# Stacked gate weights, joined score matmuls, three value chunks and a spread recurrence in a hybrid decoder trunk

## The chip, the core and the metric

The kernel runs on one core of a Trainium2 chip. The metric is the device time of one execution in microseconds (us); lower is better. The core has TensorE (PE: matmuls, and PEld: the loads of their stationary operand), VectorE (DVE), ScalarE (ACT), GpSimd (POOL) and SyncE (SP), which issues nearly all transfers. Each engine runs its own instructions in their order and waits on semaphores for the others.

## The reference

Two layers over 256 tokens of 1024 features, all in float32. The stage that the change touches lies between two feed-forward blocks of 2816 hidden features:

```python
h = rms_norm(x, mix_norm[i])
rx, rgate, q, k, v, f_logit, ga, gb = jnp.split(h @ w_in[i], split_idx, axis=-1)
# branch A: recurrence (16 blocks of 64 features)
rx = causal_dwconv(rx, conv_w[i], conv_b[i])                  # 4 taps
r  = sigmoid(block_diag(rx, rg_wa) + rg_ba);  ig = sigmoid(block_diag(rx, rg_wx) + rg_bx)
a  = exp(-8 * r * softplus(-lambda));  u = sqrt(1 - a*a) * ig * rx
ya = (scan(a, u) * gelu(rgate)) @ w_rnn_out[i]                # h_t = a_t h_(t-1) + u_t
# branch B: 8 heads of 128, causal, with a cumulative forget bias
s  = (q . k) / sqrt(128) + dcum[query] - dcum[key]            # q, k normalised per head
yb = (softmax(s, causal) @ v) @ w_attn_out[i]
x  = x + (sigmoid(ga + mb_a) * ya + sigmoid(gb + mb_b) * yb) @ w_o[i]
```

## The kernel before

**Precision.** Every operand of a matmul is split in two rounded parts, high and low, and a product is the sum of three: high by high, high by low and low by high. `mm3` (lines 303 to 306) issues the three as single matmuls. For the largest projections `mm2` puts the activation's two parts side by side, 512 columns, so that the high weight meets both in one matmul and the low weight meets the high part in another (lines 344 to 347).

**Weights.** Class `Weights` walks a plan, one list of chunks for the whole program. A chunk of about 1 MB goes by one transfer on SyncE's queue into one of 3 raw buffers (line 84). It is cut in two units, and of each unit ScalarE makes the high part `wh` (line 95) and VectorE the low part `wl` (line 96), with 5 buffers for either. A call of `next()` hands out a unit and emits the pair four units ahead. A unit feeds some 2.8 us of matmuls. A later chunk of the plan needs a raw buffer that both its units' pairs have left.

**Order.** Work that may be late is put into a list (`defer`), and `tick()` takes steps from it between units. The program is then scheduled: instructions keep their dependencies, but the scheduler sets each engine's order by its own model of time, except where `keep_in_program_order` pins one.

**The mixing stage**, once per layer, in order of the plan:

1. Eight projections of the recurrence's input (`rx_post`, lines 511 to 524): a convolution of four taps on VectorE, then a split of the result into `xch` and `xcl` (lines 522, 523).
2. Values (lines 579 to 605): four chunks of 258 columns, 1024 values and the 8 forget logits together; for each chunk 8 feature tiles times 2 token tiles times 3 matmuls. Behind chunks two, three and four stand the block-diagonal matmuls of `gates` (lines 548 to 567), 2 gates times 3 matmuls for each of 8 feature tiles; tiles 5 to 7 stand within the next stage. Two tanh on ScalarE give the two gates. Step `s1` clamps one (line 559) and makes `a`, `th` and `a2`; `s2` forms the two factors of `u` on VectorE (lines 565, 566).
3. Queries and keys of heads 0 to 3 (`qk_group`, 16 matmuls of 512 columns times 3 for each of queries and keys), then, after a `drain`, one square root over all eight tiles (`root`, line 570), and queries and keys of heads 4 to 7. In its first four units the eight products and scans (`scan`, lines 575, 576) are called two by two.
4. 24 projections called fillers (`filler`, line 754 on): eight for the gelu, eight for merge gate A, eight for B, in that order. Between the units stand the steps of the attention: `step_a` transposes one head's queries and keys and splits them, `step_b` makes scores (lines 704 to 711) and softmax, `step_c` transposes the probabilities, `step_d` applies them to the values. The head h begins at slot 4 + (5h+1)//2, where slots 0 to 7 are the second queries-and-keys group and 8 to 31 the fillers.
5. The two output projections `ya` and `yb`, the merge, and `w_o`.

**Scores before.** Tokens are two blocks of 128. Block 0 sees 128 keys and block 1 sees 256; each takes three matmuls by `mm3` and a fourth that adds both forget biases, the query's and the key's, through an operand that ScalarE builds for each head (line 702). Scores carry the opposite sign, so softmax takes the minimum; a query's own bias shifts a whole row of scores.

## Time and profile before

| what | value |
|---|---|
| median of 3 runs | 1322.99 us (1322.97 to 1323.11) |
| the profiled execution's own time | 1323.63 us |
| its span, first to last instruction | 1321.8 us |
| mean granted TensorE clock | 0.997 of full |
| busy: PE, DVE, ACT | 1311.8, 1076.1, 815.5 us |
| matmuls | 8610 |
| mixing stages of the two layers, about | 198 to 413 and 850 to 1064 us |

A group row reads: line, engine, operation, written tile <- read tiles, shapes, count | busy us, mean ns of one | idle time of the engine ahead of it and who ended it. A row of stretches reads: from:to, length, then for PE, PEld, DVE, ACT and POOL the busy us (and instructions), the granted clock, the share of the DMA engines and GB/s. Matmuls overlap their successors, so the distance between two matmuls comes from start times and not from the length of one.

### The profile page before, as it was taken

How to read it: one execution, taken by the hardware profiler on the slowest of the kernel's cores; microseconds unless marked ns; L12 is line 12 of the kernel's file. 1: busy time of each engine (PE TensorE's matmuls, PEld its weight loads, DVE VectorE, ACT ScalarE, POOL GpSimd, SP SyncE). 2: the span in 40 equal slices, each digit the busy share in tenths (PEclk: the TensorE clock that was granted, in tenths of full speed). 3: DMA queues.
4: the chain of work that ended last, by engine and by line, in shares of the span. 5: the costliest groups of instructions: out<-in, count | busy, mean ns of one | idle time of the engine just before them, and what ended most of it. 6: DMA issues, size and time to landing. Idle time of an engine off the chain costs nothing.

```text
span 1321.8 us, 22442 instructions
## 1 busy us (share of the span) xinstructions
PE 1311.8 (99%) x8610; PEld 1197.7 (91%) x8610; DVE 1076.1 (81%) x2142; ACT 815.5 (62%) x1470; POOL 34.1 (3%) x43
## 2 busy tenths in 40 slices
PE   9999999999999999999999999999999999999997
PEld 8888899889999888889988888998999998888897
DVE  7998769899757899876789877698997678988756
ACT  6665656868655666565566555578677556655653
POOL 1000000020000000000000000000200000000000
PEclk9999999999999999999999999999999999999998
DMA  8654665445435555456545546644543455554650
GB/s 292 243 179 160 212 225 193 158 164 175 151 128 191 196 189 189 162 184 231 187 165 192 188 153 212 241 161 159 193 166 128 161 190 191 192 191 142 213 187 33
DMA packets 37259, 240.21 MB, mean 182 GB/s; under 512 B 4128, under 2 KB 4768, under 8 KB 14368
## 3 DMA queue, kind: packets, MB, share of 16 engines
q1 hardware_dynamic: 36720, 238.25, 51.3%
q8 instruction: 68, 1.11, 0.3%
q10 hardware_dynamic: 432, 0.52, 0.1%
q14 instruction: 39, 0.32, 0.1%
HBM read 237.71 MB, written 1.05 MB: 181 GB/s over the span
## 4 chain that ended last, share of the span: by engine, by line
PE 99%; DMA 0%; DVE 0%; ACT 0%; SPq 0%; POOLq 0%; issue 0%; DVEq 0%
PE mm L347 20%; PE mm L345 11%; PE at L347 11%; PE at L345 6%; PE f L304 3%; PE f L305 3%; PE f L306 3%; PE qk L309 2%; PE qk L311 2%; PE qk L310 2%; PE mm L306 2%; PE mm L304 2%; PE mm L305 2%; PE ya L347 2%; PE mm L344 2%; PE at L344 2%
## 5 line engine op out<-in xcount | busy, mean ns | idle before, releaser
L95 ACT ACTIVATE wh<-wr 128x1024 fp32r<-128x1024 f32 (+2 forms) x476 | 467.4, 986 | 308.0 <-PE mm L347 90.8
L96 DVE TENSOR_TENSOR wl<-wr,wh 128x1024 fp32r<-128x1024 f32 (+2 forms) x476 | 537.7, 1132 | 142.3 <-ACT wh L95 136.9
L347 PE MATMUL mm<-h,wh 128*128 128x512 f32 x616 | 219.2, 394 | 0.0
L347 PE MATMUL at<-h,wh 128*128 128x512 f32 x616 | 218.4, 394 | 0.0
L345 PE MATMUL mm<-h,wl 128*128 128x256 f32 x704 | 182.4, 281 | 0.0
L345 PE MATMUL at<-h,wl 128*128 128x256 f32 x704 | 181.7, 281 | 0.3 <-DVE wl L96 0.2
L347 PE MATMUL mm<-f,wh 128*128 128x512 f32 x504 | 176.8, 394 | 0.0
L345 PE MATMUL mm<-f,wl 128*128 128x256 f32 x528 | 144.0, 280 | 0.0
L345 PEld LDWEIGHTS at<-h,wl 128*128 128x128 f32 x704 | 131.8, 188 | 8.8 <-DVE wl L96 0.8
L345 PEld LDWEIGHTS mm<-h,wl 128*128 128x128 f32 x704 | 131.8, 188 | 7.8 <-DVE wl L96 0.4
L347 PEld LDWEIGHTS mm<-h,wh 128*128 128x128 f32 x616 | 115.6, 188 | 22.5
L347 PEld LDWEIGHTS at<-h,wh 128*128 128x128 f32 x616 | 114.9, 188 | 21.9
L347 PEld LDWEIGHTS mm<-f,wh 128*128 128x128 f32 x504 | 94.4, 188 | 20.8
L304 PE MATMUL f<-h,wh 128*128 128x256 f32 x384 | 108.6, 283 | 0.0
L306 PE MATMUL f<-h,wl 128*128 128x256 f32 x384 | 108.4, 282 | 0.0
L305 PE MATMUL f<-h,wh 128*128 128x256 f32 x384 | 108.4, 282 | 0.0
L345 PEld LDWEIGHTS mm<-f,wl 128*128 128x128 f32 x528 | 99.4, 188 | 2.1
L305 PEld LDWEIGHTS f<-h,wh 128*128 128x128 f32 x384 | 72.3, 188 | 0.1
L304 PEld LDWEIGHTS f<-h,wh 128*128 128x128 f32 x384 | 72.3, 188 | 0.1
L306 PEld LDWEIGHTS f<-h,wl 128*128 128x128 f32 x384 | 72.4, 189 | 0.0
L381 ACT ACTIVATE sum<-mm 128x256 f32<-128x256 f32 x112 | 40.2, 376 | 49.3 <-PE mm L347 49.3
L382 DVE TENSOR_TENSOR sum<-mm,sum 128x256 f32<-128x256 f32 x112 | 44.9, 417 | 15.0 <-ACT sum L381 15.0
(291 smaller groups left out, 2857.6 us busy)
## 6 DMA issues: line engine op xcount, KB each, us to landing
wr<-in_w2i SPq DMA_DIRECT2D x44, 1024.0 KB, 4.8
wr<-in_w1i SPq DMA_DIRECT2D x41, 1024.0 KB, 4.8
wr<-in_wf SPq DMA_DIRECT2D x32, 1024.0 KB, 4.8
wr<-in_w1o SPq DMA_DIRECT2D x32, 704.0 KB, 4.0
wr<-in_w2o SPq DMA_DIRECT2D x32, 704.0 KB, 4.0
wr<-in_wqk SPq DMA_DIRECT2D x16, 1024.0 KB, 4.8
wr<-in_wv SPq DMA_DIRECT2D x8, 1032.0 KB, 4.9
wr<-in_wro SPq DMA_DIRECT2D x8, 1024.0 KB, 4.8
```

Of the source, the lines that this page charges most:

```text
L95: self.nc.scalar.activation(out=hi[:, c], in_=src[:, c], func=AF.Copy)
L96: self.nc.vector.tensor_tensor(out=lo[:, c], in0=src[:, c], in1=hi[:, c].bitcast(F32), op=ALU.subtract)
L304: T.matmul(ps, lhsT=wh, rhs=xh, start=first, stop=False)
L305: T.matmul(ps, lhsT=wh, rhs=xl, start=False, stop=False)
L306: T.matmul(ps, lhsT=wl, rhs=xh, start=False, stop=last)
L309: T.matmul(ps, lhsT=xh, rhs=wh, start=first, stop=False)
L310: T.matmul(ps, lhsT=xh, rhs=wl, start=False, stop=False)
L344: T.matmul(ps, lhsT=wh, rhs=t, start=True, stop=False, skip_group_check=True)
L345: T.matmul(ps[:, 0:S], lhsT=wl, rhs=t[:, 0:S], start=False, stop=False, skip_group_check=True)
L347: T.matmul(ps, lhsT=wh, rhs=t, start=False, stop=last, skip_group_check=True)
L381: A.activation(out=o, in_=ps[:, S:], func=AF.Copy)
L382: V.tensor_tensor(out=o, in0=ps[:, 0:S], in1=o, op=ALU.add)
```

## The change

**Gate weights stacked.** The split of the convolved input goes into two tiles: in the first the lower 64 partitions hold the high part of block 0 and the upper 64 its low part, in the second the upper hold the high part of block 1 and the lower its low part. The gate weights are laid out likewise, with one block's two gates as the 128 output columns, so that one matmul with the high weights sums high by high and low by high, and a second with the low weights adds the rest (it also adds low by low, which was left out before). Of each block's result one half is the wanted gate in its place and the other half the other gate at the wrong partitions; two transfers of 64 partitions by 256 columns per tile bring those to their place, SBUF to SBUF, on SyncE's queue.

**Scores joined.** The high query of block 0 meets high and low keys in one matmul; block 1 takes three of 256 columns; the low query of block 0 meets 128 high keys. One last matmul over 384 columns adds the key's forget bias alone to both blocks; its stationary operand is one column of a constant, repeated. The product with the low keys of block 0 lands beside its scores, and VectorE adds it with the mask ahead of the minimum (`m0`). ScalarE's operand per head is gone, as are the constants that served it.

**Values** come in three chunks of 344 columns; a weight unit holds three feature tiles of 344 instead of four of 258. Gates follow behind each of the three chunks, tiles 0 to 4, and as before 5 to 7.

**Recurrence.** The square root is called in the first group's keys part, and the eight products and scans one per unit from there on. The attention's first slot is 8 instead of 4. The fillers of the gelu and of merge gate A come in turn, two and two, and the plan of the weights with them.

```diff
-VC = 258
+NV3 = 3
+VC = 344
+AT0 = 8
...
-        plan += [(wv[l, c], [4 * VC, 4 * VC]) for c in range(4)]
+        plan += [(wv[l, c], [3 * VC, 3 * VC]) for c in range(4)]
...
-        plan += [(wf[l, f, c], [1024, 1024]) for f in (1, 2, 3) for c in range(4)]
+        plan += [(wf[l, f, c], [1024, 1024]) for c in range(4) for f in (1, 2)]
+        plan += [(wf[l, 3, c], [1024, 1024]) for c in range(4)]
...
+        xs = [big([P, KT, S], F32R, "xs") for _ in range(2)]
+        lower, upper = slice(0, 64), slice(64, P)
...
             def split():
-                A.activation(out=xch[:, m], in_=xc[:, m], func=AF.Copy)
-                V.tensor_tensor(out=xcl[:, m], in0=xc[:, m], in1=xch[:, m].bitcast(F32), op=ALU.subtract)
+                for b, own, other in ((0, lower, upper), (1, upper, lower)):
+                    A.activation(out=xs[b][own, m], in_=xc[own, m], func=AF.Copy)
+                    V.tensor_tensor(out=xs[b][other, m], in0=xc[own, m], in1=xs[b][own, m].bitcast(F32),
+                                    op=ALU.subtract)
...
-            for g in range(2):
-                c = slice((m * 2 + g) * P, (m * 2 + g + 1) * P)
-                mm3(ps[:, g * S:(g + 1) * S], wg_hi[:, c], wg_lo[:, c], xch[:, m], xcl[:, m], True, True)
+            for b in range(2):
+                c = slice((m * 2 + b) * P, (m * 2 + b + 1) * P)
+                T.matmul(ps[:, b * S:(b + 1) * S], lhsT=wg_hi[:, c], rhs=xs[b][:, m], start=True, stop=False)
+                T.matmul(ps[:, b * S:(b + 1) * S], lhsT=wg_lo[:, c], rhs=xs[b][:, m], start=False, stop=True)
...
+            for b, own, other in ((0, lower, upper), (1, upper, lower)):
+                c = slice(b * S, (b + 1) * S)
+                A.activation(out=t2[:, c], in_=ps[:, c], func=AF.Tanh, scale=0.5, bias=hcol(l, ("ba", "bx")[b], m))
+                nc.sync.dma_start(out=thi[own], in_=t2[other, c])
...
-                V.tensor_scalar(out=thr, in0=thr, scalar1=-1.0, scalar2=None, op0=ALU.max)
+                for b, own in ((0, lower), (1, upper)):
+                    V.tensor_scalar(out=thr[own], in0=t2[own, b * S:(b + 1) * S], scalar1=-1.0, scalar2=None,
+                                    op0=ALU.max)
...
-            V.tensor_tensor(out=tq[:, m], in0=tq[:, m], in1=xc[:, m], op=ALU.mult)
+            tc.keep_in_program_order(V.tensor_tensor(out=tq[:, m], in0=tq[:, m], in1=xc[:, m], op=ALU.mult))
...
+                if w == 1 and u == 1:
+                    while len(ready) < KT:
+                        tick()
+                    root()
+                if w == 1 and u > 1:
+                    scan(u - 2)
...
-            for t, o, nk in ((0, 0, P), (1, P, S)):
-                q = slice(t * P, (t + 1) * P)
-                mm3(ps[:, o:o + nk], qh[:, q], ql[:, q], kh[:, 0:nk], kl[:, 0:nk], True, False)
-                T.matmul(ps[:, o:o + nk], lhsT=bl[:, q], rhs=dk[:, 0:nk], start=False, stop=True)
+            mm(slice(0, S), qh[:, q1], kk[:, 1], start=True)
+            mm(slice(0, S), qh[:, q1], kk[:, 0])
+            mm(slice(0, S), ql[:, q1], kk[:, 0])
+            mm(slice(S, 2 * S), qh[:, q0], kk[:, :, q0])
+            mm(slice(S, S + P), ql[:, q0], kk[:, 0, q0])
+            mm(slice(0, S + P), pick[:, h:h + 1].to_broadcast([P, P]), dk, stop=True)
...
+            V.tensor_tensor(out=m0[:, q0], in0=ps[:, S + P:], in1=mask[:, q1], op=ALU.add)
...
-                slots[4 + (5 * h + 1) // 2 + i].append((f, h))
+                slots[AT0 + (5 * h + 1) // 2 + i].append((f, h))
...
-        for f in range(3 * KT):
+        turns = [f + m for m in range(0, KT, 2) for f in (0, 1, KT, KT + 1)] + list(range(2 * KT, 3 * KT))
+        for i, f in enumerate(turns):
```

What the scheduler makes of it, at three places. The tile numbers in these rows are the program's own; line numbers of the changed kernel differ.

SyncE's queue around the chunks of queries and keys (`in_wqk`) of layer 0, before:

```order
L84 DMA wr43_2598<-in_wv 128x2064
L84 DMA wr44_2694<-in_wqk 128x2048
L84 DMA wr45_2796<-in_wqk 128x2048
L84 DMA wr46_2890<-in_wqk 128x2048
L84 DMA wr47_2967<-in_wqk 128x2048
L84 DMA wr48_3044<-in_wqk 128x2048
```

and now, where `thi<-tg` is a pair of moves of one tile's half gates:

```order
L86 DMA wr45_2767<-in_wqk 128x2048
L558 DMA thi212_2614<-tg215_2617 64x256 x2
L558 DMA thi218_2628<-tg221_2631 64x256 x2
L86 DMA wr46_2851<-in_wqk 128x2048
L558 DMA thi226_2724<-tg229_2727 64x256 x2
L558 DMA thi232_2738<-tg235_2741 64x256 x2
L86 DMA wr47_2927<-in_wqk 128x2048
L86 DMA wr48_3013<-in_wqk 128x2048
L558 DMA thi240_2832<-tg243_2835 64x256 x2
L86 DMA wr49_3060<-in_wqk 128x2048
L558 DMA thi250_2875<-tg253_2878 64x256 x2
```

The moves stand in the same queue as the weight chunks, each behind the chunk above it and ahead of the chunk below.

VectorE at the first two gates of layer 0 (`thr` is the clamp, `xc<-thi` the product with the other gate, `wl` a weight's low part), before:

```order
L96 TENSOR_TENSOR wl88_2697<-wr44_2694,wh88_2696 128x1024
L523 TENSOR_TENSOR xcl186_2207<-xc184_2205,xch185_2206 128x256
L518 SCALAR_TENSOR_TENSOR xc184_2205<-rxp0_102,vt_71,xc184_2205 128x256
L559 TENSOR_SCALAR thr213_2667<-thr213_2667 128x256
L566 SCALAR_TENSOR_TENSOR xc184_2205<-thi214_2668,xc184_2205 128x256
L559 TENSOR_SCALAR thr218_2680<-thr218_2680 128x256
L566 SCALAR_TENSOR_TENSOR xc184_2205<-thi219_2681,xc184_2205 128x256
```

and now:

```order
L563 TENSOR_SCALAR thr211_2613<-tg215_2617 64x256 x2
L512 SCALAR_TENSOR_TENSOR xc184_2195<-rxp2_102,vt_71,xc184_2195 128x256
L98 TENSOR_TENSOR wl87_2652<-wr43_2586,wh87_2651 128x1032
L571 SCALAR_TENSOR_TENSOR xc184_2195<-thi212_2614,xc184_2195 128x256
L507 TENSOR_TENSOR rxp1_101<-at202_2481,RB197_2308 128x256
L571 SCALAR_TENSOR_TENSOR xc184_2195<-thi218_2628,xc184_2195 128x256
L512 SCALAR_TENSOR_TENSOR xc184_2195<-rxp0_100,vt_71,xc184_2195 128x256
L98 TENSOR_TENSOR wl88_2683<-wr44_2680,wh88_2682 128x1024
```

The product no longer follows its clamp at once: a convolution step and a weight's low part stand between, and the next weight's low part stands behind the product.

TensorE at the scores of head 4 of layer 0, before, with the transposes of the probabilities of head 3 (`pt`) inside:

```order
L304 MATMUL s389_3880<-aq380_3825,aq378_3823 128x128
L729 MATMUL pt383_3833<-ident_89,pr371_3767 128x128 x2
L305 MATMUL s389_3880<-aq381_3826,aq378_3823 128x128
L306 MATMUL s389_3880<-aq380_3825,aq379_3824 128x128
L711 MATMUL s389_3880<-dk242_2886,aq382_3827 128x128
L304 MATMUL s389_3880<-aq380_3825,aq378_3823 128x256
L305 MATMUL s389_3880<-aq381_3826,aq378_3823 128x256
L306 MATMUL s389_3880<-aq380_3825,aq379_3824 128x256
L711 MATMUL s389_3880<-dk242_2886,aq382_3827 128x256
```

and now one head's scores (`s418`), with the output of an earlier head (`o`) ahead of them and the transposes of a later head's queries and keys (`tr`) behind:

```order
L759 MATMUL o414_4079<-ph405_4024,vl206_2522 128x128
L721 MATMUL s418_4127<-ak413_4074,aq411_4072 128x256 x2
L721 MATMUL s418_4127<-ak413_4074,aq412_4073 128x256
L721 MATMUL s418_4127<-ak413_4074,aq411_4072 128x256
L721 MATMUL s418_4127<-ak413_4074,aq412_4073 128x128
L721 MATMUL s418_4127<-dk244_2847,pick_97 128x384
L702 MATMUL tr425_4178<-ident_89,qk289_3129 128x128 x4
```

Eight matmuls have become six, and only one of them has fewer than 256 columns.

More of the change, by code (lines that the diff above doesn't have):

```diff
@@ L201, in trunk @@
     tri = cp.tile([P, S], F32R, name="tri")
-    acol = cp.tile([P, NH], F32, name="acol")
-    mcol = cp.tile([P, NH], F32, name="mcol")
-    grp = cp.tile([P, 4], F32, name="grp")
-    sel = cp.tile([P, 3], F32, name="sel")
+    neglo = cp.tile([P, 1], F32, name="neglo")
+    pick = cp.tile([P, NH], F32R, name="pick")
     lfh = cp.tile([P, TT, P], F32R, name="lfh")
@@ L247, in constants @@
         yield
-        V.tensor_tensor(out=acol, in0=ident[:, 0:NH], in1=ident[:, 32:32 + NH], op=ALU.add)
-        V.tensor_tensor(out=mcol, in0=ident[:, 64:64 + NH], in1=ident[:, 96:96 + NH], op=ALU.add)
-        V.tensor_scalar(out=mcol, in0=mcol, scalar1=-1.0, scalar2=None, op0=ALU.mult)
-        yield
-        for g in range(4):
-            V.tensor_reduce(out=grp[:, g:g + 1], in_=ident[:, 32 * g:32 * g + 32], axis=AX.X, op=ALU.add)
-        yield
-        V.tensor_tensor(out=sel[:, 0:1], in0=grp[:, 1:2], in1=grp[:, 3:4], op=ALU.add)
-        V.tensor_scalar(out=sel[:, 0:1], in0=sel[:, 0:1], scalar1=-1.0, scalar2=None, op0=ALU.mult)
-        V.tensor_tensor(out=sel[:, 1:2], in0=grp[:, 0:1], in1=grp[:, 1:2], op=ALU.add)
-        V.tensor_tensor(out=sel[:, 2:3], in0=grp[:, 2:3], in1=grp[:, 3:4], op=ALU.add)
+        V.tensor_tensor(out=pick, in0=ident[:, 0:NH], in1=ident[:, 32:32 + NH], op=ALU.add)
+        V.tensor_reduce(out=neglo, in_=ident[:, 32:64], axis=AX.X, op=ALU.add)
+        V.tensor_scalar(out=neglo, in0=neglo, scalar1=-1.0, scalar2=None, op0=ALU.mult)
         yield
@@ L506, in mix @@
         xc = big([P, KT, S], F32, "xc")
-        xch = big([P, KT, S], F32R, "xch")
-        xcl = big([P, KT, S], F32R, "xcl")
+        xs = [big([P, KT, S], F32R, "xs") for _ in range(2)]
+        lower, upper = slice(0, 64), slice(64, P)
         def rx_post(m, ps):
@@ L629, in forget @@
             A.activation(out=dh, in_=dps[:, 0:S], func=AF.Copy)
[L630 to L633 removed]
+            for o, n_ in ((0, S), (S, P)):
+                V.scalar_tensor_tensor(out=dk[:, o:o + n_], in0=dh[:, 0:n_].bitcast(F32), scalar=neglo,
+                                       in1=dps[:, 0:n_], op0=ALU.mult, op1=ALU.add)
         qk = [None, None]
@@ L679, in mix @@
         drain()
-        root()
         yr, ot = Pair("yr"), Pair("ot")
@@ L701, in step_a, with mm @@
             V.scalar_tensor_tensor(out=kl, in0=ps[:, S:], scalar=g, in1=kh.bitcast(F32), op0=ALU.mult, op1=ALU.subtract)
-            A.activation(out=s["b"], in_=dc.bitcast(F32), func=AF.Identity, scale=mcol[:, h:h + 1], bias=acol[:, h:h + 1])
         def step_b(h):
             s = st[h]
-            (qh, ql), (kh, kl), bl = s["q"], s["k"], s["b"]
+            (qh, ql), kk = s["q"], s["k"]
+            q0, q1 = slice(0, P), slice(P, S)
             ps = atbank("s")
-            for t, o, nk in ((0, 0, P), (1, P, S)):
-                q = slice(t * P, (t + 1) * P)
-                mm3(ps[:, o:o + nk], qh[:, q], ql[:, q], kh[:, 0:nk], kl[:, 0:nk], True, False)
-                T.matmul(ps[:, o:o + nk], lhsT=bl[:, q], rhs=dk[:, 0:nk], start=False, stop=True)
+            def mm(o, w, r, start=False, stop=False):
+                T.matmul(ps[:, o], lhsT=w, rhs=r, start=start, stop=stop, skip_group_check=True)
+            mm(slice(0, S), qh[:, q1], kk[:, 1], start=True)
[4 more added lines that the diff above has]
+            mm(slice(0, S + P), pick[:, h:h + 1].to_broadcast([P, P]), dk, stop=True)
             sv = pr = awork(384, "pr", 2, F32)
             mx, rs = small(TT, "mx", "sa"), small(TT, "rs", "sa")
-            for t, o, nk in ((0, 0, P), (1, P, S)):
-                V.tensor_tensor_reduce(out=sv[:, o:o + nk], in0=ps[:, o:o + nk], in1=mask[:, S - nk:S], scale=1.0,
+            m0 = work(s="m0")
+            V.tensor_tensor(out=m0[:, q0], in0=ps[:, S + P:], in1=mask[:, q1], op=ALU.add)
+            for t, o, nk, pc, mk in ((0, 0, P, slice(S, S + P), m0[:, q0]), (1, P, S, slice(0, S), mask)):
+                V.tensor_tensor_reduce(out=sv[:, o:o + nk], in0=ps[:, pc], in1=mk, scale=1.0,
                                        scalar=3e38, op0=ALU.add, op1=ALU.min, accum_out=mx[:, t:t + 1])
@@ L1000, in _layout @@
     put("mbb", g["merge_b"][:, D:])
-    put("ba", g["rg_ba"])
-    put("bx", g["rg_bx"])
+    rb, ib = (g[n].reshape(L, KT, 2, 64) for n in ("rg_ba", "rg_bx"))
+    put("ba", np.concatenate([rb[:, :, 0], ib[:, :, 0]], axis=2))
+    put("bx", np.concatenate([ib[:, :, 1], rb[:, :, 1]], axis=2))
     put("pb", g["ple_b_gate"])
```

68 lines of the change are left out of this document (32 added, 36 removed).

## The prediction

> **What bounds the kernel now.** I read the page's head and its chain of waits first, then who TensorE waits for, then single stretches of the mixing stage, the only one that the change touches.
>
> ```profile
> span 1321.8 us, 22442 instructions
> PE 1311.8 (99%) x8610; PEld 1197.7 (91%) x8610; DVE 1076.1 (81%) x2142; ACT 815.5 (62%) x1470; POOL 34.1 (3%) x43
> PE 99%; DMA 0%; DVE 0%; ACT 0%; SPq 0%; POOLq 0%; issue 0%; DVEq 0%
> ...
> PE warm L871 <- POOL ones L189: 1.1, 1, 1.1
> PE fin L933 <- DVE xg L931: 0.9, 1, 0.9
> PE st L927 <- DVE facc L923: 0.4, 1, 0.4
> PE at L345 <- DVE wl L96: 0.2, 1, 0.2
> ```
>
> A matmul's busy time covers its pipelined tail, so 99% proves little alone. The wait list (waiter, what it waited for, total us, times, longest) does: 1.1 at the start, 1.3 at the end, and 0.2 us for a weight in between. The time is the number of matmuls times the distance between their starts. Shortening another engine's work cannot gain anything; only fewer or shorter matmuls can, and a new wait loses only once it has eaten the lead that the other engines hold.
>
> **The distance between matmuls**, from start times of the TensorE timeline (start, us of one, line, tile): a chunk of values (48 matmuls of 258 columns by the code) between two groups of gates, the gates ahead of it (12 of 256), and six matmuls of 512.
>
> ```profile
> 226.81 0.28 PE L304 MATMUL g<-xch,wbh 128*128 128x256 f32 x1
> ...
> 228.22 0.28 PE L309 MATMUL v<-wh,h 128*128 128x258 f32 x1
> ...
> 233.96 0.28 PE L304 MATMUL g<-xch,wbh 128*128 128x256 f32 x1
> ...
> 263.19 0.40 PE L309 MATMUL qk<-wh,h 128*128 128x512 f32 x1
> ...
> 264.57 0.40 PE L309 MATMUL qk<-wh,h 128*128 128x512 f32 x1
> ```
>
> (228.22 − 226.81)/12 = 0.1175 us at 256 columns; (233.96 − 228.22)/48 = 0.1196 at 258; (264.57 − 263.19)/6 = 0.230 at 512. From 256 to 512 that is 0.44 ns a column and about 5 ns for each matmul besides.
>
> **The change, part by part.** The counts of what goes (one row stands for each of three or four equal ones):
>
> ```profile
> L304 PE MATMUL g<-xch,wbh 128*128 128x256 f32 x32 | 9.0, 280 | 0.0
> L309 PE MATMUL v<-wh,h 128*128 128x258 f32 x128 | 36.2, 283 | 0.0
> L304 PE MATMUL s<-aq,aq 128*128 128x256 f32 x16 | 5.3, 333 | 0.0
> ```
>
> Gates: three matmuls become two, because high and low parts are stacked on the two halves of the array. 32 of 96 go: 32 × 0.1175 = 3.8 us. This is the firmest term.
>
> Values: 3 × 128 = 384 of 258 columns become 288 of 344, the same columns in all. The trace has no 344. Along the slope it is 0.1196 + 86 × 0.00044 = 0.157, so 384 × 0.1196 − 288 × 0.157 = 45.9 − 45.3 = 0.6 us; at the rate of a whole 512 (0.230 × 344/512 = 0.1545) it is 45.9 − 44.5 = 1.4. I take 0.8, nearer the slope, whose foot is the same stage.
>
> Scores: for each of 16 heads four matmuls of 128 columns and four of 256 become four of 256, one of 128 and one of 384, again the same columns. One head before (its first score matmul stands among transposes):
>
> ```profile
> 344.05 0.31 PE L304 MATMUL s<-aq,aq 128*128 128x128 f32 x1
> ...
> 344.36 0.31 PE L305 MATMUL s<-aq,aq 128*128 128x128 f32 x1
> ...
> 344.72 0.33 PE L304 MATMUL s<-aq,aq 128*128 128x256 f32 x1
> 344.90 0.28 PE L305 MATMUL s<-aq,aq 128*128 128x256 f32 x1
> ...
> 345.25 0.28 PE L305 MATMUL f<-h,wh 128*128 128x256 f32 x1
> ```
>
> Three of 128 take 344.72 − 344.36 = 0.36, so 0.12 each, as much as 256 columns: short matmuls pay a floor. The first 256 behind them takes 0.18. The head costs 0.89 + 0.12 = 1.01 us. After: 4 × 0.1175 + 0.12 + 0.174 (384 on the slope) = 0.76, or 0.82 if the 0.06 behind a short matmul stays. The gain is 0.19 to 0.25; I take 0.20 a head, 3.2 us. The stationary operand of the last matmul is one column repeated 128 times, which no row shows; the loads of the scores take 190 ns and those of the transposes 140, all hidden, and if this one took twice 190 and showed fully it would cost 16 × 0.19 = 3.0 us. I take zero, since a load that is hidden has nothing to gain either, and keep 3.0 for the range's upper end.
>
> The sum is 3.8 + 0.8 + 3.2 = **7.8 us**. The profiled execution took 1323.63, so 1315.8; the median shown is 1322.99, 0.64 lower, so **1315.2 us**.
>
> What else is added lies on VectorE, ScalarE and SyncE's queue.
>
> ```profile
> L523 DVE TENSOR_TENSOR xcl<-xc,xch 128x256 fp32r<-128x256 f32 x16 | 6.7, 417 | 0.0
> L559 DVE TENSOR_SCALAR thr<-thr 128x256 f32<-128x256 f32 x16 | 4.6, 287 | 0.0
> L598 DVE SCALAR_TENSOR_TENSOR vl<-v,R,vh 128x258 fp32r<-128x258 f32 x16 | 7.7, 482 | 2.0 <-ACT vh L597 1.7
> L715 DVE CUSTOM_DVE_ANT_0 pr<-s,mask 128x128 f32<-128x128 f32 x16 | 4.5, 284 | 1.4 <-PE s L711 1.4
> L702 ACT ACTIVATE aq<-dc,acol,mcol 128x256 fp32r<-128x256 f32 x16 | 9.6, 599 | 0.0
> ...
> core 0: us, PE busy (x) PEld busy (x) DVE busy (x) ACT busy (x) POOL busy (x), PEclk, DMA share, GB/s
> 226.00:249.00 23.00, 23.00 (x172) 21.93 (x171) 20.24 (x48) 21.38 (x47) 0.00 (x0) 1.00 0.44 143
> 249.00:272.00 23.00, 23.00 (x106) 18.82 (x105) 18.11 (x43) 18.36 (x28) 2.02 (x2) 1.00 0.48 177
> 272.00:295.00 23.00, 23.00 (x127) 19.65 (x126) 22.69 (x40) 13.08 (x17) 7.33 (x5) 1.00 0.44 152
> ...
> 374.00:400.00 26.00, 26.00 (x173) 23.76 (x173) 14.84 (x26) 12.94 (x24) 0.00 (x0) 1.00 0.37 133
> ```
>
> Per layer VectorE gets 8 more splits on half the partitions (if partitions don't shorten an operation, 8 × 0.417 = 3.3 us) and 8 more clamps (8 × 0.287 = 2.3); two evictions fewer but wider ones give back some 0.4. That is 5.2 us in the two stretches from 226 to 272, where it was idle 46 − 38.35 = 7.65. The masked half-scores (8 × about 0.284 = 2.3) come with the attention, which starts four units later and so reaches into 374 to 400, idle 11 us. ScalarE gets 8 × 0.41 and loses 8 × 0.599. The cover of all this is the weights' lead:
>
> ```profile
> ACT wh L95 <- PE qk L311: 13.0, 16, 1.8
> SPq L84 <- DVE wl L96: 387.5, 87, 13.7
> ...
> 268.49 2.44 DVE L575 TENSOR_TENSOR tq<-tq,xc 128x256 f32<-128x256 f32 x7 [2.09 <-ACT tq L570]
> ...
> 271.45 3.01 DVE L576 TENSOR_TENSOR_SCAN xc<-a,tq 128x256 f32<-128x256 f32 x5
> 274.37 1.20 DVE L96 TENSOR_TENSOR wl<-wr,wh 128x1024 fp32r<-128x1024 f32 x1
> ```
>
> ScalarE waits for the matmul that frees the pair's buffer, so a pair is made as early as five buffers allow: four units, here 4 × 12 × 0.230 = 11.0 us, ahead of use. Spreading the recurrence takes apart the burst of the last three rows (a wait for the square root, then products and scans with no weight pair until 274.37). TensorE waited nowhere there, so the pacing by itself is worth nothing; it only keeps the lead large. The gelu and merge-gate projections in turn do the same for the VectorE load behind. Fewer constants at the start sit ahead of the first landing and count as nothing.
>
> **Rivals.** (1) Only columns count. Values and scores keep theirs (49,536 per layer and 1,536 per head), so only the gates gain: 1322.99 − 3.8 = 1319.2. For it: the 5 ns beside the slope is small and read from few rows. Against: 0.12 us at 128 columns. The Trainium skill (TensorE: Matmul & The Clock Gate, Back-to-back issue gap) has the isolated gap as columns over 2.4 GHz plus 2.5 ns; an estimate by it gives 0.2 us for the values, 0.1 for the scores and 3.5 for the gates, 1319.2 as well, but this trace's 0.230 at 512 and 0.12 at 128 do not agree with it.
>
> (2) The other side: the moves of half a gate starve TensorE. Each gate now sends two 64-partition pieces from SBUF to SBUF through SyncE, and VectorE's product with them waits for the landing, with the weight pairs queued behind it.
>
> ```profile
> wr<-in_wqk SPq DMA_DIRECT2D x16, 1024.0 KB, 4.8
> ...
> out_dram<-out SPq DMA_DIRECT2D x2, 128.0 KB, 2.1
> ```
>
> The nearest small transfer lands in 2.1 us; behind a weight chunk just issued it would be 4.8 + 2.1 = 6.9. In the changed order a clamp pair, a convolution step and a weight pair stand between, with ScalarE's two tanh of the next gate and its copy: about 3 us from tanh to product. So a gate costs nothing at best and 4 at worst. VectorE can lose 2.4 idle + 11.0 lead = 13.4 us a layer, 1.7 for each of 8 gates, before TensorE waits; from there every microsecond counts. At 3.0 a gate it is 24 − 13.4 = 10.6 a layer: 1315.2 + 21 = 1336. For it: in SyncE's changed order the moves of five of the eight gates stand right behind a chunk. Against: the DMA engines are busy 0.44 to 0.48 of that stretch, so mostly nothing is ahead; and a chunk delayed behind a move has its own lead (SyncE waited up to 13.7 us for buffers). The Trainium skill (DMA: Bandwidth & Descriptors, Queues, rings and completion order) says that descriptors on each engine are consumed in ring order, which would be the 6.9; no run here yet shows it for such a move.
>
> (3) The attention, four units later, ends nearer to the output projection that reads it, and short waits for softmax or the last head come back: say 2.8 us a layer, a softmax chain's few operations, 1320.8. Against: scores and transposes keep about as many matmuls between them as before. (4) The recurrence isn't really spread because the scheduler moves it back: the order shows that it is spread, and the time would be the forecast's anyway.
>
> **How the numbers follow.** Forecast 0.76, (1) 0.08, (3) 0.10, (2) 0.06. A measurement here can't tell less than 0.2%, 2.6 us, from no change: 1320.3 to 1325.6. The forecast, (1) and the shorter waits of (3) are faster, 0.86; the rest of (3) is the same, 0.08; (2) is slower, 0.06. The likeliest one's own range goes from 1313.5 (gains of 3.8 + 1.4 + 4.0, 9.2) to 1318.0 (3.0 for the repeated column). For 8 in 10 I take 1313.0 to 1319.5, with (1) inside and most of (2) and (3) left out.
>
> **What would show it.** TensorE's instructions fall by 96 + 32 + 32 = 160 to about 8450; waits of TensorE stay under 2 us in the mixing stage; starts of value matmuls are 0.155 to 0.158 apart; a head's scores take 0.76 to 0.82. Wrong if TensorE waits for a weight pair between 215 and 300 with VectorE idle ahead of the product with the moved half (then (2)), if scores show gaps at the repeated column, or if the value matmuls are 0.160 apart or more.

## The result and the profile after

| | before | changed |
|---|---|---|
| median | 1323.05 us (1322.97 to 1323.30) | 1337.01 us (1335.97 to 1337.62, 4 runs) |
| ratio to before | | 1.0104, 95% interval 1.0089 to 1.0119 |
| span of the profiled execution | 1321.8 us | 1334.2 us |
| matmuls | 8610 | 8450 |

The change makes the kernel 14 us slower where a gain of 7.8 was forecast. The head of the page of the changed kernel, its chain of waits by engine, and the list of what TensorE waited for (waiter, what it waited for, total us, times, longest):

```profile
span 1334.2 us, 22258 instructions
PE 1309.7 (98%) x8450; PEld 1191.6 (89%) x8450; DVE 1091.3 (82%) x2178; ACT 813.6 (61%) x1466; POOL 34.1 (3%) x43
...
PE 92%; DVE 4%; ACT 2%; issue 1%; DMA 0%; POOL 0%; SPq 0%; POOLq 0%; DVEq 0%
...
PE f L297 <- DVE g L777: 8.9, 10, 1.4
PE ya L337 <- DVE g L777: 3.6, 2, 1.8
...
PE at L338 <- DVE wl L98: 0.5, 2, 0.3
...
PE at L337 <- ACT wh L97: 0.4, 1, 0.4
```

Two things can be read at once. The 160 matmuls are gone, as they should be. And the chain, which before was TensorE's for 99%, now passes through VectorE for 4% and ScalarE for 2%: TensorE waits 8.9 + 3.6 = 12.5 us for one operation, `g<-f` of line 777, with which VectorE takes a filler's result out of its PSUM bank. Nothing of the kind stood in the list before. (The chain's shares alone would not do: 94%, 3% and 1% stand in the fastest run below too, where these waits are all but gone.) The weights, whose lead the prediction counted as the cover, are waited for 0.5 + 0.4 us, all of it in the first 9 us of the program, and in neither mixing stage. When each distance between two starts on TensorE is set against the usual distance of its kind and only what is over 0.15 us above it is added up, before comes to 3.2 us and the changed kernel to 21.2: **18.0 us of new loss**. It lies between 292 and 381 us in the first layer and between 950 and 1043 in the second. All but 1.2 us of it is waits. The 1.2 us are matmuls that start late one after the other behind the last and longest wait, of 1.82 us, though nothing is waited for: from 1039.1 to 1042.5 us the granted clock is at half (in a row of stretches the third number from the end).

```profile
1035.00:1039.00 4.00, 2.18 (x15) 1.80 (x15) 3.31 (x10) 2.12 (x5) 0.00 (x0) 1.00 0.72 262
1039.00:1042.50 3.50, 3.50 (x12) 2.95 (x11) 1.03 (x5) 1.56 (x7) 0.00 (x0) 0.51 0.00 0
```

One of the waits, on TensorE. The first row is the last matmul of a filler (24 matmuls each); 16 us later the filler four places behind it, which needs the same bank, cannot start (a bracket shows idle time and who ended it):

```profile
323.26 0.28 PE L299 MATMUL f<-h,wl 128*128 128x256 f32 x1
...
337.54 0.39 PE L721 MATMUL s<-dk,pick 128*128 128x384 f32 x1
...
339.76 0.39 PE L297 MATMUL f<-h,wh 128*128 128x256 f32 x1 [1.39 <-DVE g L777]
```

and VectorE at the same place:

```profile
337.61 1.22 DVE L98 TENSOR_TENSOR wl<-wr,wh 128x1024 fp32r<-128x1024 f32 x1 [1.41 <-ACT wh L97]
338.76 0.28 DVE L731 TENSOR_TENSOR m<-s,mask 128x128 f32<-128x128 f32 x1
338.96 0.41 DVE L328 TENSOR_TENSOR ot<-o,ot 128x256 fp32r<-128x256 f32 x1
339.29 0.75 DVE L777 TENSOR_TENSOR g<-f,RB 128x256 f32<-128x256 f32 x2
```

The filler was complete at 323.5 and is taken out at 339.3, together with the next one, behind `m<-s`, the masked half of a head's scores, which TensorE finished only at 337.9, and one operation on an earlier head's output (`ot`). VectorE was not short of time: it sat idle for 1.41 us just ahead. The fillers have four banks, so a result may lie some three fillers long; before, VectorE stood waiting for the filler rather than the other way round, and took it out at once:

```profile
335.69 0.42 DVE L759 TENSOR_TENSOR g<-f,RB 128x256 f32<-128x256 f32 x1 [0.15 <-PE f L306]
```

Over the 24 fillers of layer 0, the time from a filler's last matmul to its eviction was 0.04 to 2.7 us before. Now, from the sixth filler on, it is 3.7 to 15.8, and four times in the layer the bank comes free less than 0.1 us before its next user starts.

The savings are there. On TensorE of the changed kernel, eight gate matmuls and then one chunk of values (48 matmuls of 344 columns) up to the next gate:

```profile
222.87 0.28 PE L550 MATMUL g<-xs,wbh 128*128 128x256 f32 x1
...
223.82 0.32 PE L302 MATMUL v<-wh,h 128*128 128x344 f32 x1
...
231.37 0.29 PE L550 MATMUL g<-xs,wbh 128*128 128x256 f32 x1
```

(223.82 − 222.87)/8 = 0.119 us a gate matmul, (231.37 − 223.82)/48 = 0.157 a value matmul. Summed over all their start distances, gates fall from 11.4 to 7.6 us and values from 46.0 to 45.4. Scores have to be taken together with the transposes that stand among them, since the distance of a short matmul depends on its neighbours (0.059 us at 128 columns between wide ones, 0.12 in a row of three): 24.5 us before, and 22.2 in the run with own buffers and heads two units apart (below), where no wait falls between them. That is 3.8 + 0.6 + 2.3 = 6.7 us. The profiled execution follows from this within about one us: 1323.63 − 6.7 + 18.0 = 1334.9, against 1335.97.

An estimate by the formula of the Trainium skill (TensorE: Matmul & The Clock Gate, Back-to-back issue gap) for the isolated gap, columns over 2.4 GHz plus 2.5 ns, is 0.146 us for 344 columns; the 0.157 here does not agree.

### The profile page after: what moved, and what is told of

It reads as the page before. It is cut to its first block, busy times and chain, and to the rows that moved or that the text cites. A ratio compares the mean times of both kernels' runs of the same rounds, so it can differ in the third digit from the quotient of the medians.

```text
span 1334.2 us, 22258 instructions
## 1 busy us (share of the span) xinstructions
PE 1309.7 (98%) x8450; PEld 1191.6 (89%) x8450; DVE 1091.3 (82%) x2178; ACT 813.6 (61%) x1466; POOL 34.1 (3%) x43
## 4 chain that ended last, share of the span: by engine, by line
PE 92%; DVE 4%; ACT 2%; issue 1%; DMA 0%; POOL 0%; SPq 0%; POOLq 0%; DVEq 0%
PE mm L340 19%; PE mm L338 11%; PE at L340 11%; PE at L338 6%; PE f L297 3%; PE f L298 3%; PE f L299 3%; PE mm L299 2%; PE mm L297 2%; PE mm L298 2%; PE ya L340 2%; PE mm L337 2%; DVE wl L98 2%; PE at L337 2%; PE o L340 1%; PE pl L297 1%
```

## Experiments

### Which part makes the evictions late

The three theories were the shared buffers of the half-scores (A), the attention's later start (B), and the fillers in turn (C); D was the joined scores as such.

**Own buffers for the half-scores:**

```diff
-            m0 = work(s="m0")
+            m0 = awork(P, "m0", 2, F32)
```

> The changed kernel with one line different: the masked half-scores (tile m) get buffers of their own, two of 128 columns, in place of one of the twelve buffers that they share with the results of the fillers (tile g). Theory A, the shared buffers: those twelve are handed out in the order in which the program names the tiles, so a filler's result that is named behind a head's half-scores can be taken out of PSUM only behind them on VectorE, however long before it was finished; the bank of that filler then comes free 6 to 16 us late. With buffers of its own the late evictions go, TensorE's waits for VectorE fall from some 19 us to under 2, and the time is what the sum of the prediction gave, 1315 to 1317. Rival B, the attention that starts four units later, and rival C, the projections in turn, are both left as they are: by them the time stays at 1334 to 1337. Rival D, the joined scores themselves (one buffer for the key's parts, two each for the query's, so the heads follow each other more tightly): 1334 to 1337 too.

Measured: 1331.19 us, ratio 1.0061 (1.0049 to 1.0074). Waits of TensorE:

```profile
PE o L337 <- DVE sum L375: 2.6, 2, 1.3
PE ya L338 <- DVE wl L98: 2.5, 4, 0.8
PE o L757 <- ACT ph L749: 2.5, 2, 1.2
PE f L297 <- DVE g L777: 1.8, 2, 0.9
```

The wait for the evictions falls from 12.5 to 1.8 us, as A said and B, C and D did not. The time does not: three other waits, at the end of the attention and behind it, have come up in their place. The mechanism is confirmed, and it was not the whole loss.

What the line does is seen in the scheduled order. VectorE in the changed kernel, the half-scores (L731, `m0`) and the evictions (L777) alone; the number behind the last underscore of a name rises in the order in which the program names the tiles:

```
L731 TENSOR_TENSOR m0383_3856<-s379_3846,mask_94 128x128
L777 TENSOR_TENSOR g385_3900<-f384_3869,RB197_2308 128x256
L777 TENSOR_TENSOR g394_3952<-f393_3923,RB197_2308 128x256
L731 TENSOR_TENSOR m0399_3965<-s395_3955,mask_94 128x128
```

and with own buffers:

```
L777 TENSOR_TENSOR g385_3900<-f384_3869,RB197_2308 128x256
L777 TENSOR_TENSOR g394_3952<-f393_3923,RB197_2308 128x256
L731 TENSOR_TENSOR m0360_3690<-s356_3680,mask_94 128x128
L777 TENSOR_TENSOR g402_4014<-f401_3983,RB197_2308 128x256
...
L777 TENSOR_TENSOR g424_4175<-f423_4146,RB197_2308 128x256
L731 TENSOR_TENSOR m0383_3856<-s379_3846,mask_94 128x128
```

In the first, `m0` and `g`, which come from the same twelve buffers, stand strictly in the order of their names; `m0383` precedes `g385` although TensorE makes the scores `s379` after fillers 384, 393, 401 and 407. In the second, `m0` stands where its scores come, and the evictions have gone ahead of it.

**That tile alone, added to the kernel before**, once shared and once in a buffer of its own. The operation's result is read by nobody:

```diff
+            m0 = work(s="m0")                  # second run: awork(P, "m0", 1, F32)
+            V.tensor_tensor(out=m0[:, 0:P], in0=ps[:, P:S], in1=mask[:, P:S], op=ALU.add)
```

> The kernel before with nothing of the change but one VectorE operation more for each head: a masked half of 128 columns of the scores, written to one of the twelve shared buffers and read by nobody. Its work is 16 times 0.28, 4.5 us of VectorE, in a stage where TensorE waits for nothing. Theory A (the shared buffers order the evictions): the fillers' evictions come late as in the changed kernel, 1323 + 8 to 16, so 1331 to 1339. Rival: an operation of 0.28 us off the bound costs nothing, 1322.5 to 1324.

> The same as the run with a shared tile, the kernel before with one VectorE operation more for each head that nobody reads, but written to a buffer of its own. Theory A: the evictions stay where they were and the time is that of before, 1322.5 to 1324. If VectorE's added work itself were the cause, the same as with the shared tile, over 1328.

Measured: 1338.35 us shared, ratio 1.0114 (1.0100 to 1.0128); 1322.95 own, ratio 1.0000 (0.9991 to 1.0009). Largest wait in a list, shared:

```profile
PE f L304 <- DVE g L761: 7.6, 6, 1.8
```

and own, where only the waits of before are left:

```profile
PE warm L873 <- POOL ones L189: 1.1, 1, 1.1
```

The same 16 operations of 0.285 us cost 15 us or nothing, according to the buffer they write to. This is the cleanest evidence: none of the other parts of the change is in it. Waits are only part of the 15 us: the list has 7.6 + 1.0 us that the kernel before has not. Behind three of them the granted clock is at half for 3.4 us, first here:

```profile
316.90:320.30 3.40, 3.18 (x15) 3.18 (x16) 3.40 (x13) 2.06 (x7) 0.00 (x0) 0.50 0.73 289
```

**More of the shared buffers:**

```diff
-        return kp.tile([P, 256], dt, name=nm(s), tag="w", bufs=12)
+        return kp.tile([P, 256], dt, name=nm(s), tag="w", bufs=14)
```

> The changed kernel with fourteen shared buffers of 256 columns in place of twelve. Theory A: the order in which the shared buffers are handed out does it, not how many there are, so the same late evictions and 1334 to 1338. Rival (too few buffers: a result waits until one is free): two more buffers let the evictions go ahead, 1316 to 1331.

Measured: 1336.46 us, ratio 1.0103 (1.0089 to 1.0116), with the wait list of the changed kernel in its first rows. So it is not that twelve buffers are too few. That the order in which they are handed out does it rests on the orders shown above and on the pair of runs with one tile more.

**The attention from unit 4, and the fillers in rows:**

```diff
-AT0 = 8
+AT0 = 4
```

> The changed kernel with the attention starting at unit 4, as before, in place of 8. Rival B (attention that ends nearer to the output projection): the waits of TensorE go, 1315 to 1321. Theory A (shared buffers): the same heads and fillers meet four units earlier, the late evictions come four fillers earlier and are as many, so 1333 to 1338. Rivals C and D: 1333 to 1338.

```diff
-        turns = [f + m for m in range(0, KT, 2) for f in (0, 1, KT, KT + 1)] + list(range(2 * KT, 3 * KT))
+        turns = list(range(3 * KT))
```

> The changed kernel with the fillers and their weights in the order of before (eight of the recurrence's gate, eight of the first merge gate, eight of the second) in place of pairs in turn. Rival C (projections in turn): merge-gate evictions have no near reader and are put off by the order; without turns 1315 to 1321. Theory A: the order of the names still puts each head's half-scores ahead of the next fillers' results, so 1333 to 1338. Rivals B and D: 1333 to 1338.

Measured: 1341.95 us, ratio 1.0143 (1.0129 to 1.0157), and 1335.53, ratio 1.0092 (1.0078 to 1.0106). The waits for the eviction are 16.3 us in the first and 10.0 + 3.4 in the second. B and C fall as causes of the late evictions. The earlier start came out 4 us slower than A expected (1333 to 1338): its longest wait for an eviction is 2.8 us, against 1.8 in the changed kernel, and the granted clock is at half four times for 3.4 us, against once.

**The scores of before in the changed kernel** (two groups, four matmuls each, no masked half):

> The changed kernel with the scores of before (two separate groups of 128 and 256 columns, decay of both sides, no masked half), all else as changed: it gives up the 3.2 us that the prediction put down for the joined scores. Theory A and rival D: the late evictions go with the half-scores, 1315.2 + 3.2 = 1318.4, between 1317 and 1320. Rivals B and C: the waits stay, 1337 + 3 = 1338 to 1341.

Measured: 1322.27 us, ratio 0.9995 (0.9985 to 1.0005). The evictions are on time (0.4 us of waits), as expected, but the time is 2.3 us over the expected range. Gates and values should gain 4.4 us there; 3.3 us of new waits, 1.0 of them in each layer ahead of `ya`, took most of that back.

### The second cause: where the heads end

**Own buffers and the attention from unit 4** (both edits above):

> The changed kernel with the half-scores in buffers of their own and the attention from unit 4 on, as before. With own buffers alone the time was 1331.19, and most of what TensorE still waited stood where the last heads meet the output projections (382 to 393 us) and in the output projection (434 us). Theory E (the second cause is the attention four units later: its last heads share VectorE, ScalarE and the weights' buffers with the projections that follow): these waits go, about 2 times 5 to 6 us, so 1318 to 1321. Theory F (the second cause is the other placing, fillers in turn and the paced recurrence): 1328 to 1332.

Measured: 1325.90 us, ratio 1.0022 (1.0013 to 1.0031). That is 5.3 us less than with own buffers alone; neither E (1318 to 1321) nor F (1328 to 1332) had the size.

**Own buffers and heads two units apart**, still from unit 8 on:

```diff
-            m0 = work(s="m0")
+            m0 = awork(P, "m0", 2, F32)
...
-                slots[AT0 + (5 * h + 1) // 2 + i].append((f, h))
+                slots[AT0 + 2 * h + i].append((f, h))
```

> The changed kernel with two lines different: the half-scores in buffers of their own, and the heads two units apart in place of two and a half, so that the last head is done at unit 25 in place of 29 although the first still starts at unit 8. Theory G (behind the shared buffers, the second cause is that the last heads run into the output projections; where the first head starts has no part in it): waits of TensorE for VectorE and ScalarE between 280 and 440 us go, and the time is 1323.0 less what the matmuls themselves showed: gates 3.8, values 0.6, scores 15.2 - 13.4 = 1.8 by the sums of start distances, so 1316.8, between 1316 and 1319. Theory E (the start four units later): 1325 to 1332. If the serial use of the key's one buffer holds the heads back: closer heads wait for each other and it is over 1331.

Measured: **1318.57 us, ratio 0.9966 (0.9953 to 0.9978)**, faster than both kernels. All that is left beyond the waits of before:

```profile
PE f L297 <- DVE g L777: 1.8, 2, 0.9
```

So the second cause is where the heads end. This is the last matmul of the last head's scores in layer 0, with own buffers alone, with own buffers and the attention from unit 4, and in this run:

```profile
388.04 0.39 PE L721 MATMUL s<-dk,pick 128*128 128x384 f32 x1
...
383.21 0.39 PE L721 MATMUL s<-dk,pick 128*128 128x384 f32 x1
...
371.34 0.39 PE L721 MATMUL s<-dk,pick 128*128 128x384 f32 x1
```

The output projections (`ya`) begin at 368.7, 369.4 and 372.2 us. In the first two runs the last heads stand among them, in the third they come before. G says that the start of the first head has no part in it, and that goes too far: starting four units earlier moved the end by 4.8 us and the time by 5.3, though by the units alone the last head of that run should end where it ends here. Nor is an end among the projections enough by itself: in the kernel before the last scores stand at 377.2 us, behind the first `ya` at 373.2, and nothing waits there.

**Heads two units apart with the shared buffers:**

> The changed kernel with the heads two units apart and the half-scores left in the twelve shared buffers: the half of the run with own buffers and two units that leaves out the buffers. Theory A: the evictions are still ordered behind the half-scores, but fewer fillers are named between two heads, so less of the bank's margin goes; some TensorE waits for VectorE's evictions remain, 1321 to 1332. If only the spacing counted: 1318 to 1319, as with own buffers.

Measured: 1323.14 us, ratio 1.0000 (0.9991 to 1.0009).

```profile
PE f L297 <- DVE g L777: 4.7, 8, 0.9
```

Closer heads alone win back 14 us, own buffers alone 6, both together 18. Theory A's reason, that with fewer fillers named between two heads less stands behind each half-score, fits the 4.7 us of waits in place of 12.5; it was not tried apart from the heads' end.

**The scans two units later**, on top of own buffers and two units:

```diff
-                if w == 1 and u > 1:
-                    scan(u - 2)
...
-                if 4 * w + u < KT - 2:
-                    scan(4 * w + u + 2)
+                scan(4 * w + u)
```

> As the run with own buffers and heads two units apart (1318.57), with the recurrence's products and scans begun two units later, one a unit over the eight units of the second query-key group. There TensorE still waited 0.9 us a layer for the first filler's eviction, at 293 us, and VectorE had no idle time from 278 to 296. If it is VectorE's load in that stretch: the wait halves or goes, 1316.8 to 1318.2. If the later scans meet the first heads and fillers instead: 1318.5 to 1322.

Measured: 1317.82 us, ratio 0.9961 (0.9947 to 0.9975), the fastest version of the study. Its wait list has `PE f` for `DVE g` at 1.2 us in place of 1.8, which speaks for VectorE's load ahead of the fillers as what remained there.

### The terms one by one

**Values alone** on the kernel before:

> The kernel before with the values in three chunks of 344 columns alone. The prediction's term: 0.8 us, between 0.6 and 1.4, so 1322.2; rival 1 (only columns count): 1323.0. No bank or weight should be waited for: the order of the fillers and the heads stays that of before.

Measured: 1322.60 us, ratio 0.9997 (0.9988 to 1.0006), no new wait. The direction is right; by time alone it can't be told from nothing, and the start distances give 0.6.

**The repeated column.** On own buffers and two units, the last matmul of the scores gets an ordinary operand; the kernel then leaves out the right forget bias and computes all else:

```diff
-            mm(slice(0, S + P), pick[:, h:h + 1].to_broadcast([P, P]), dk, stop=True)
+            mm(slice(0, S + P), lfh[:, 0], dk, stop=True)
```

> As the run with own buffers and heads two units apart, but the scores' last matmul has an ordinary stationary operand of 128 columns in place of one column repeated 128 times, so the forget gate's decay is not what it should be; the matmul has 384 columns still. If the repeated column is what makes it 0.228 us in place of the 0.174 of the slope, its distance falls to about 0.174 and the time by 16 x 0.054 = 0.9 us. If not, 0.228 stays and the time is the same within 0.5 us.

Measured: 1318.79 us against 1318.57. With the ordinary operand, and with the repeated column:

```profile
335.80 0.39 PE L721 MATMUL s<-dk,lfh 128*128 128x384 f32 x1
336.03 0.28 PE L298 MATMUL f<-h,wh 128*128 128x256 f32 x1
```

```profile
335.89 0.39 PE L721 MATMUL s<-dk,pick 128*128 128x384 f32 x1
336.12 0.28 PE L298 MATMUL f<-h,wh 128*128 128x256 f32 x1
```

0.23 in both. The repeated column costs nothing, and 384 columns take 0.228 here and not the 0.174 of the slope. Why is open.

**The gates alone** on the kernel before:

> The kernel before with the stacked gates alone (two matmuls in place of three, half gates moved by transfers). The prediction's term: 3.8 us, 1319.2. If the moves starve TensorE (rival 2 of the prediction): over 1323. If the shifted order alone makes the query-key bank come free late, as in the run with the three savings on the old schedule, where the first filler waited 9.4 us a layer: 1320 to 1335, with the wait ahead of the first filler at about 287 and 940 us.

Measured: 1335.16 us, ratio 1.0091 (1.0077 to 1.0104). The term that the prediction called the firmest loses 12 us by itself. Waits of TensorE:

```profile
PE f L304 <- DVE qk L672: 7.6, 2, 3.8
PE s L305 <- DVE aq L710: 3.1, 2, 1.6
```

and VectorE (`dk` is the end of the forget gate's work, L584 the recurrence's products, with the scans behind them up to 291.0, `qk<-qk` frees a query-key bank):

```profile
270.40 0.41 DVE L641 TENSOR_SCALAR dk<-dc,sel 128x256 fp32r<-128x256 f32 x1
...
278.69 1.77 DVE L584 TENSOR_TENSOR tq<-tq,xc 128x256 f32<-128x256 f32 x5 [2.86 <-ACT tq L579]
...
293.42 0.70 DVE L672 TENSOR_TENSOR qk<-qk,s 128x512 f32<-128x512 f32 x1
```

The burst of the recurrence, which stood at 268.5 before, has moved ten us later, onto the query-key banks that the fillers wait for. The stand costs more than its length, as the stretch behind it shows:

```profile
293.30:300.20 6.90, 6.03 (x28) 6.03 (x29) 5.88 (x18) 1.41 (x5) 3.25 (x3) 0.51 0.46 167
```

and matmuls of 256 columns 0.21 us apart behind the wait, in place of 0.118:

```profile
294.17 0.58 PE L304 MATMUL f<-h,wh 128*128 128x256 f32 x1 [3.79 <-DVE qk L672]
...
294.77 0.41 PE L306 MATMUL f<-h,wl 128*128 128x256 f32 x1
294.98 0.41 PE L304 MATMUL f<-h,wh 128*128 128x256 f32 x1
```

Once TensorE has stood 1.6 + 3.8 = 5.4 us in two pieces, its granted clock is at 0.50 up to 300.2 us. 24 of the 28 matmuls there have 256 columns, and 0.21 us in place of 0.118 makes 2.2 us more for them. The Trainium skill (TensorE: Matmul & The Clock Gate, What's actually happening) says that after an idle window of about 3.4 us the clock is at half; this trace agrees with the half, by its 0.50 behind the 3.8 us. The changed kernel does not agree with the length, since its clock went to half behind 1.82 us.

**The three savings on the old schedule**, with own buffers:

> The kernel before with only the three savings: stacked gates, values in three chunks, joined scores with the half-scores in buffers of their own; the attention's start, the order of fillers and weights and the recurrence's place are those of before. Theories E and F alike: no late evictions and no tail, so the sum of the prediction comes out, 1315.2, between 1314 and 1318. If the savings themselves were mis-sized (a matmul of 384 columns showed 0.228 us in place of 0.174, some 0.9 us in all), 1316 to 1317. If every moved order costs some waits, 1319 to 1325.

Measured: 1340.16 us, ratio 1.0127 (1.0109 to 1.0145), far from every expectation. One wait of 9.4 us a layer, at the same bank:

```profile
PE f L295 <- DVE qk L661: 18.7, 2, 9.4
```

**The gates with the paced recurrence** on the kernel before:

> The kernel before with the stacked gates and the paced recurrence (square root after the second weight pair of the keys' first group, then one product and scan a unit), all else as before. With the gates alone TensorE stood 5.7 us a layer at 287 to 294 us, behind a query-key bank that VectorE freed late: seven products and eight scans of the recurrence, with weight pairs between them, stand ahead of it from 278.7 to 291 us, and the granted clock was 0.50 and 0.73 in the eight us after it. Theory H (the burst of the recurrence, which the gates push ten us later, onto that bank): the wait at 287 goes and the granted clock stays at 1.00; the time falls from 1335 to 1319.2 if nothing else is late, or to 1323 to 1331 if the last heads, two and a half units apart, run into the output projections as in the run with own buffers. Rival (the gates' other VectorE work, the half-partition splits and clamps): the wait at 287 stays, 1333 to 1336.

Measured: 1339.78 us, ratio 1.0128 (1.0114 to 1.0141). The wait at 287 is gone, but the scans now meet the bank before it, at 281 (`PE qk`), and the tail is back:

```profile
PE qk L309 <- DVE qk L675: 6.1, 2, 3.0
PE o L756 <- ACT ph L748: 2.6, 3, 1.2
```

Slower than expected (1323 to 1331 with the tail). H named work that does stand ahead of the bank (scans at 281.2, 282.1 and 283.4 us, the eviction at 284.1), but pacing does not keep it off the bank by itself.

**The recurrence as before, on own buffers and two units:**

> The kernel of the run with own buffers and heads two units apart (1318.57), with the recurrence where it was before: square root after the drain, products and scans two by two in the first four units of the second query-key group, unpinned. Theory H (with the stacked gates the burst of products and scans meets the query-key bank, as in the runs with the gates alone and with the parts on the old schedule, and the pacing is what holds that off): a wait of 4 to 10 us a layer at 281 to 294 us, 1327 to 1341. The prediction's reading (the pacing by itself is worth nothing): 1317.5 to 1320.

Measured: 1319.89 us, ratio 0.9977 (0.9968 to 0.9987).

```profile
PE qk L302 <- DVE qk L667: 3.2, 2, 1.6
```

H expected 1327 to 1341 and falls in this form: pacing is worth 1.3 us here. The same burst does little harm because it comes early. VectorE in this run:

```profile
266.65 0.43 DVE L581 TENSOR_TENSOR tq<-tq,xc 128x256 f32<-128x256 f32 x1 [1.70 <-ACT tq L576]
...
294.95 0.73 DVE L636 SCALAR_TENSOR_TENSOR dk<-dh,neglo,dc 128x256 fp32r<-128x256 f32 x2
```

The recurrence starts at 266.7 and `dk` comes at 295, while with the gates alone `dk` came first, at 270.4, and the recurrence at 278.7. The changed kernel calls the forget gate's work two units later, behind the last gates, a line of the change that its description leaves out, and the three kernels on the old schedule that lost time at the query-key banks do not. That this is what holds the burst off is an inference from these two orders, in kernels that differ in more than that; it was not tried by itself and stays open.

**The gates of before, on own buffers and two units:**

> The kernel of the run with own buffers and heads two units apart (1318.57), with the gates of before: three matmuls on full 128 rows, no moves of half gates. It measures the gates' term where no bank is late: 1318.57 + 3.8 = 1322.4 by the prediction's term, less what the waits before the fillers give back (up to 2 us), so 1320.4 to 1322.6. If the stacked gates cost as much elsewhere as they save: 1318 to 1319.

Measured: 1320.89 us, ratio 0.9984 (0.9975 to 0.9993). Where little is late, the stacked gates gain 1320.89 − 1318.57 = 2.3 us, as expected: TensorE's 3.8 less 1.5. That is near the 1.8 us that TensorE waits for VectorE ahead of the fillers in the version with stacked gates.

## Why the prediction was wrong, point by point

**What bounds the kernel:** right for the kernel before. The sentence built on it, that a new wait "loses only once it has eaten the lead that the other engines hold", was taken as the weights' lead alone. That lead held (no wait for a weight in either mixing stage). The lead that was eaten is a second one, four PSUM banks between the fillers and VectorE, which the prediction neither named nor priced.

**The step that failed** is the one on the added VectorE work: "The masked half-scores (8 × about 0.284 = 2.3) come with the attention". It set an operation's length against idle time. The operation was indeed 0.284 us and VectorE had the time; it cost 15 us by itself (1338.35 against 1322.95), because it writes to a buffer of the pool from which the fillers' results come, so that it fixes the order of the evictions. The order of VectorE around this operation could have been looked at: its rows stand in the order of the names. The prediction showed TensorE's order there, and only VectorE's around the gates. Two more steps failed with it: that the attention's later end costs nothing, and that a part which saves matmul time saves as much by itself. None of the prediction's signs of being wrong appeared: no wait for a weight between 215 and 300 us, no gap at the repeated column, value matmuls 0.157 apart, and single waits under 2 us, of which there were many.

**Gates**, 3.8 us: right as matmul time (11.4 to 7.6), wrong as a gain by itself. Alone the stacked gates lost 12 us, and where little else is late they gain 2.3. **Values**, 0.8: 0.6 by start distances, and the 0.157 on the slope was right. **Scores**, 3.2: mis-sized; with the transposes among them they gain 2.3, 0.14 a head in place of 0.20. The term's weak point was 0.174 for 384 columns, which measured 0.228. (The expectations above put 1.8, from the scores' own start distances.) The sum of the terms is 6.7 in place of 7.8. (By the prediction's own figures its likeliest range is 1322.99 − 9.2 = 1313.8 to 1315.2 + 3.0 = 1318.2, not 1313.5 to 1318.0; nothing hangs on it.)

**The repeated column** at zero: right, by experiment. **The pacing**, which "by itself is worth nothing": 1.3 us in the version without late banks. **Fillers in turn**: undone, the changed kernel showed 1335.53 against 1337.01, so next to nothing, as said.

**Rivals.** (1) falls by the start distances: values and scores gain 0.6 and 2.3 us with the same columns. (2) did not happen: VectorE waited once, for 0.5 us, for the moves of half gates, which landed in 3.2 us at the median (the second row; 64 KB each), not in 6.9.

```profile
DVE xc L571 <- DMA thi<-tg: 0.5, 1, 0.5
...
thi<-tg SPq DMA_DIRECT2D x32, 64.0 KB, 3.2
```

Its side, slower, and even about its time, 1336, came out by luck, by another mechanism. (3) named a true cause, the attention's end near the output projections, at 2.8 us a layer. With own buffers in place, starting four units earlier removed (1331.19 − 1325.90)/2 = 2.6 a layer, near that price, and closer heads (1331.19 − 1318.57)/2 = 6.3; with the shared buffers the earlier start lost 5 us more. The rival's counter-argument, as many matmuls between scores and transposes as before, looked at TensorE's order and not at who empties the banks. (4) The recurrence was spread, and the time was not the forecast's.

## What to carry to other kernels

Beside the lead of what an engine reads, price the lead of what it writes: how many result banks there are, how long one may lie, and which instruction on the evicting engine stands ahead of the eviction. Where a scheduler sets the order, an added operation is costed by what its buffer and its place do to that order, not by its length, so the evicting engine's order around each added operation is to be read before its cost is put at nothing. A tile that is written late does not belong in a rotating pool that feeds a bank's eviction.

## What the runs showed of the hardware that was not expected

- Short waits lower the clock. In these traces the granted clock changes in steps of 3.41 us. Set against these steps, in the mixing stages of nineteen of the twenty traces, a step at full clock in which TensorE sat idle for 1.70 us or more was followed by one at 0.50 in 15 of 16 cases, and a step with 1.64 us or less never (the twentieth trace shows 0.75 throughout). The same wait of 1.82 us halved the clock in the second layer of the changed kernel, where all of it fell into one step, and not in the first, where 1.54 us of it did. At 0.50, matmuls of 256 columns went from 0.118 to 0.21 us.
- A matmul of 384 columns, the last of a head's scores, took 0.228 us, as much as one of 512 (0.230), and 344 columns took 0.157, on the line between 256 and 512. The stationary operand, one column repeated or 128 columns, made no difference.
- A matmul of 128 columns between wide ones took 0.059 us, where three in a row took 0.12 each.
